# T1 and T3 of the seven-product pairs formed by accumulating DMA, and a fourth such pair per chunk

## The chip, the cores and the metric

The kernel runs on one core of a Trainium2 chip. The core has a matmul engine (TensorE; PE in the profile), an elementwise engine (VectorE; DVE), an activation engine (ScalarE; ACT), a general engine (GpSimd; POOL) and a queue engine that mostly issues DMAs (SyncE; SP). Each takes its own instructions in order and waits for the others by semaphores. The metric is the device time of one execution in microseconds; the time before is the median of three runs, 1666.11 us.

## The reference

One layer of a hybrid encoder on 256 rows of 2048 channels in float32: two attention branches, gated and merged, then a SwiGLU feed-forward part, then a norm. The change lies in the feed-forward part:

```
h2 = rmsnorm(x, ffn_norm_g)
x = x + (silu(h2 @ w_ffn_gate) * (h2 @ w_ffn_up)) @ w_ffn_down     # 2048 -> 5632 -> 2048
return rmsnorm(x, final_norm_g)
```

## The kernel before

A float32 product is made of three float32r products: each operand is split in a high part (ScalarE casts it, line 92) and a low part (VectorE subtracts, line 93), and `mm3` (lines 174 to 178) multiplies high by high, high by low and low by high. So each weight that is loaded costs a cast on ScalarE and a subtraction on VectorE before TensorE may use it.

The feed-forward part runs over 11 chunks of 512 hidden columns, in parts of 4, 4 and 3 chunks; after each part the down projection adds that part's share to the output. Inside a chunk, `hidden` (line 684) goes over 8 pairs of 128-row blocks of the 2048 input channels. For a pair there are four weight blocks of 128x512, stored side by side: the gate block of the first rows (g0), the up block of the second (u1), the up block of the first (u0) and the gate block of the second (g1).

A plain pair (`plain_weights`, line 638) loads these in two transfers of 512 KB, splits each in two operations of 128x1024 per engine, and multiplies in 24 matmuls of 512 columns (2 halves of the rows x 4 weights x 3). A pair in `SEVEN` (pairs 0, 2 and 4) takes the seven products of a Strassen-like scheme instead of eight, so 21 matmuls. For that the sums T1 = g0 + u0, T3 = u1 + u0, T2 = T1 + u1 and T4 = T2 + g1 of weights are formed on VectorE (lines 645 to 647) and split like weights; the sums of the activations (h2S) are made once. After the last such pair the seven accumulators are recombined (lines 699 to 703, four operations on VectorE), while the plain pairs that follow run on. `between` (line 691), called before pair 6, transposes the hidden values of the chunk before.

Slots are handed out by tile pools with tags: `raw` (6 slots, loaded weights), `w` (8 slots, split weights), `t` (5 slots, the sums, and the split g0, u1 and g1 of a seven-product pair). A slot is written again when its last reader is done. The order of each engine's instructions is set by a scheduler at build time, by its own timeline.

Of the kernel before, what the change touches and what calls it, by code (L numbers as in the profile page):

```python
# [8 lines left out]
F32 = mybir.dt.float32  # L9
F32R = mybir.dt.float32r  # L10
AF = mybir.ActivationFunctionType
ALU = mybir.AluOpType
AX = mybir.AxisListType

P = 128
# [14 lines left out]
G_END = 42  # L30

NF = 11
SEVEN = (0, 2, 4)

C_ID, C_DIST, C_COS, C_SIN, C_END = 0, 128, 512, 640, 768

# [2 lines left out]
def hybrid_block(ctx: ExitStack, tc: tile.TileContext, x, xT, gains, w_lat, w_kr, w_dqk, w_dv, w_g0, w_g1, b_gate,  # L39
                 w_qn, w_qr, w_kn, w_v, lq1, lk1, lq2, lk2, diff_norm_g, w_mla, w_diff, w_out, w_gu, w_fd,  # L40
                 final_norm_g, consts, out):
    nc = tc.nc
# [4 lines left out]
    wp = ctx.enter_context(tc.tile_pool(name="wp", bufs=1))  # L47
# [7 lines left out]
    def nm(s):  # L55
        n_tile[0] += 1
        return f"{s}_{n_tile[0]}"

    def lt(dt=F32, shape=(P, 2, S)):
        return up.tile(list(shape), dt, tag="L", name=nm("L"), bufs=48)  # L60
# [28 lines left out]
    def split(src, hi, lo, scale=None):  # L89

        if scale is None:
            nc.scalar.copy(hi, src)  # L92
            nc.vector.tensor_tensor(out=lo, in0=src, in1=hi.bitcast(F32), op=ALU.subtract)  # L93
        else:
            nc.scalar.activation(out=hi, in_=src, func=AF.Copy, scale=scale)
            nc.vector.scalar_tensor_tensor(out=lo, in0=src, scalar=scale, in1=hi.bitcast(F32),  # L96
                                           op0=ALU.mult, op1=ALU.subtract)
# [76 lines left out]
    def mm3(o, l, r, start, stop):  # L174

        nc.tensor.matmul(o, lhsT=l[0], rhs=r[0], start=start, stop=False)  # L176
        nc.tensor.matmul(o, lhsT=l[0], rhs=r[1], start=False, stop=False)  # L177
        nc.tensor.matmul(o, lhsT=l[1], rhs=r[0], start=False, stop=stop)  # L178
# [378 lines left out]
    for c in range(4):  # L557
        z, t = [lt(shape=(P, 512)) for _ in range(2)], [lt(shape=(P, 512)) for _ in range(2)]
# [12 lines left out]
    def sums_of(tp, gs):  # L571

        a, t = nt((P, 2, S)), nt((P, 4, P))
        for j in range(2):
            nc.scalar.activation(out=a[:, j], in_=tp[:, j], func=AF.Copy, scale=gs[j])
        a11, a12, a21, a22 = a[:, 0, 0:P], a[:, 1, 0:P], a[:, 0, P:S], a[:, 1, P:S]
        nc.vector.tensor_tensor(out=t[:, 0], in0=a21, in1=a22, op=ALU.subtract)
        nc.vector.tensor_tensor(out=t[:, 1], in0=a11, in1=a21, op=ALU.subtract)
        nc.vector.tensor_tensor(out=t[:, 2], in0=t[:, 0], in1=a11, op=ALU.subtract)
        nc.vector.tensor_tensor(out=t[:, 3], in0=a12, in1=t[:, 2], op=ALU.add)  # L580
        hi, lo = lt(F32R, (P, 4, P)), lt(F32R, (P, 4, P))
        split(t, hi, lo)
        return hi, lo

    x2ss = const.tile([P, 8], F32, name="x2ss")
    for c in range(4):
        o = project(mT, w_out, c)
        z = []
        for h in range(2):
            xr = nt()  # L590
            nc.sync.dma_start(out=xr, in_=x[0, h * P:(h + 1) * P, c * 512:(c + 1) * 512])
            t = lt(shape=(P, 512))
# [4 lines left out]
        for j0 in range(0, 4, 2):  # L597
# [5 lines left out]
            pair = 2 * c + j0 // 2  # L603
            if pair in SEVEN:
                h2S[pair] = sums_of(tp, gs)
# [10 lines left out]
    fp = ctx.enter_context(tc.tile_pool(name="fp", bufs=1, reuse_waits="tile"))  # L616
    fq = ctx.enter_context(tc.tile_pool(name="fq", bufs=1, space=bass.MemoryType.PSUM, reuse_waits="tile"))

    def bank(role, shape=(P, 512)):
        return fq.tile(list(shape), F32, tag=f"q{role}", name=nm("q"), bufs=1)  # L620

    def load(src):
        raw = wp.tile([P, 2, 512], F32, tag="raw", name=nm("raw"), bufs=6)
        nc.sync.dma_start(out=raw, in_=src)
        return raw
# [2 lines left out]
        return wp.tile([P, 2, 512], F32R, tag="w", name=nm("w"), bufs=8)  # L628

    def extra(dt=F32R):  # L630
        return fp.tile([P, 2, 512], dt, tag="t", name=nm("t"), bufs=5)

    def parts_of(src, alloc):
        hi, lo = alloc(), alloc()
        split(src, hi, lo)
        return [(hi[:, j], lo[:, j]) for j in range(2)]
# [3 lines left out]

    def seven_weights(src):

        a, b = load(src[:, 0:2]), load(src[:, 2:4])
        t13, t24 = extra(F32), extra(F32)
        nc.vector.tensor_tensor(out=t13, in0=a, in1=b[:, 0:1].broadcast_to([P, 2, 512]), op=ALU.add)
        nc.vector.tensor_tensor(out=t24[:, 0], in0=t13[:, 0], in1=a[:, 1], op=ALU.add)
        nc.vector.tensor_tensor(out=t24[:, 1], in0=t24[:, 0], in1=b[:, 1], op=ALU.add)
        w = {}
        w[1], w[3] = parts_of(a, extra)
        b21 = extra()  # L650
        split(b[:, 1], b21[:, 0], b21[:, 1])
        w[2] = b21[:, 0], b21[:, 1]
        w[5], w[7] = parts_of(t13, two)
        w[6], w[4] = parts_of(t24, two)
        return w
# [5 lines left out]
    def seven_products(q, pair, w, start, stop):  # L661

        hi, lo = h2S[pair]
        s1, s3, s2, s4 = [(hi[:, j], lo[:, j]) for j in range(4)]
        a0, a1 = h2T[2 * pair], h2T[2 * pair + 1]
        ls = {1: part_of(a0, 0), 2: part_of(a1, 0), 3: s4, 4: part_of(a1, 1), 5: s1, 6: s2, 7: s3}
        for i in (1, 5, 7, 6, 2, 3, 4) if start else (1, 3, 2, 5, 7, 6, 4):
            mm3(q[i], ls[i], w[i], start, stop and i in (1, 5, 6, 7))
# [15 lines left out]
    def hidden(c, between):  # L684

        pairs = len(h2T) // 2
        last = max(SEVEN) if SEVEN else None
        q, base = {}, None
        for p in range(pairs):
            if p == pairs - 2:  # L690
                between()
            if p in SEVEN:
                w = seven_weights(w_gu[c, p])
                if not q:
                    q = {i: bank(i) for i in (1, 5, 7, 6, 2, 3, 4)}
                seven_products(q, p, w, p == min(SEVEN), p == last)
                if p == last:
                    c1, v2, v3, d12, d22 = (sc() for _ in range(5))
                    nc.scalar.copy(c1, q[1])
                    nc.vector.tensor_tensor(out=v2, in0=c1, in1=q[6], op=ALU.add)  # L700
                    nc.vector.tensor_tensor(out=d12, in0=q[5], in1=v2, op=ALU.subtract)
                    nc.vector.tensor_tensor(out=v3, in0=q[7], in1=v2, op=ALU.add)
                    nc.vector.tensor_tensor(out=d22, in0=q[5], in1=v3, op=ALU.subtract)
                    base = ((c1, d12), (v3, d22))
                continue
            g0_, u1, u0, g1_ = plain_weights(w_gu[c, p])
            if 8 not in q:
                q[8] = bank(8)
            if not SEVEN and not p:
                q.update({i: bank(i) for i in (2, 3, 4)})  # L710
            for a, (wg, wu) in ((h2T[2 * p], (g0_, u0)), (h2T[2 * p + 1], (g1_, u1))):
                first_k = a is h2T[0]
                for h, (i, j) in enumerate(((2, 3), (4, 8))):
                    l = part_of(a, h)
                    end = a is h2T[-1]
                    mm3(q[i], l, wg, first_k, end)
                    mm3(q[j], l, wu, first_k or (j == 8 and SEVEN and p == 1 and a is h2T[2]), end)
        f = []
# [55 lines left out]
    for m in range(a, b):  # L774
        for j in range(4):
            if j % 2 == 0:
                raw = load(w_fd[3, m][:, j:j + 2])
# [104 lines left out]
```

## Time and profile before

| | us |
|---|---|
| median of three runs (lowest, highest) | 1666.11 (1664.88, 1667.57) |
| the profiled execution | 1665.36 |
| its span, first to last instruction | 1663.6 |
| PE busy in the span | 1648.0 (99%) |
| DVE busy | 1158.8 (70%) |
| ACT busy | 845.2 (51%) |
| POOL busy | 26.2 (2%) |

The engines work beside each other, so busy times don't add up. The chain of waits follows the work back from the last instruction and says which engine held the end at each moment. The windows cut the span in stretches and give each engine's busy time in them. A group row gives how often a form of an operation ran, its busy time and mean length, and the engine's idle time just before. Operations of one engine may overlap, so a mean length can be more than the distance from one start to the next, which the timeline shows.

### The profile page before, as it was taken

The numbers are of one execution on the slowest core, as the hardware profiler recorded it, in microseconds if no ns is written. First come the engines' busy times: TensorE is split into PE (matmuls) and PEld (weight loads), VectorE is DVE, ScalarE is ACT, GpSimd is POOL, SyncE is SP. The second block draws the span as 40 slices with busy tenths as digits, with TensorE's granted clock in tenths as the row PEclk, the third lists the DMA queues.
The fourth block names the chain that finished last, engine by engine and source line by source line (L and its number), as shares of the span: only waits on it lengthen the run. The fifth ranks groups of instructions, "written<-read, shape, count | busy, mean of one in ns | idle before, by whom it ended". The sixth has DMA issues, their size and how long they took to land.

```text
span 1663.6 us, 22367 instructions
## 1 busy us (share of the span) xinstructions
PE 1648.0 (99%) x8443; PEld 1407.1 (85%) x8443; DVE 1158.8 (70%) x1490; ACT 845.2 (51%) x1158; POOL 26.2 (2%) x49
## 2 busy tenths in 40 slices
PE   8999999999999999999999999999999999999998
PEld 7888888888888999998888788888888888888886
DVE  7676665666555766765656889975679885688865
ACT  6465554455444666565445555544445554445543
POOL 0000000010000000000000000000000000000010
PEclk9999999999999999999999999999999999999999
DMA  9655555466666545556766566666566655566662
GB/s 329 222 176 168 175 176 178 153 197 203 213 209 197 180 159 176 169 170 207 237 213 207 176 192 197 206 202 202 190 202 202 199 189 196 186 203 203 197 221 103
DMA packets 99133, 323.67 MB, mean 195 GB/s; under 512 B 10960, under 2 KB 17104, under 8 KB 99024
## 3 DMA queue, kind: packets, MB, share of 16 engines
q1 hardware_dynamic: 98880, 322.22, 58.7%
q8 instruction: 66, 1.08, 0.3%
q14 instruction: 43, 0.35, 0.1%
q10 hardware_dynamic: 144, 0.02, 0.0%
HBM read 315.91 MB, written 6.29 MB: 194 GB/s over the span
## 4 chain that ended last, share of the span: by engine, by line
PE 97%; DMA 1%; DVE 1%; ACT 0%; issue 0%; SPq 0%; ACTq 0%; POOLq 0%; POOL 0%; DVEq 0%
PE q L176 14%; PE q L177 14%; PE q L178 14%; PE mm L176 12%; PE mm L177 12%; PE mm L178 12%; PE mm L201 9%; PE mm L202 5%; PE ps L178 1%; PE ps L177 1%; PE ps L176 1%; PE q L677 1%; PE ps L108 1%; DMA raw<-in_w_dqk_dram 1%; DMA raw<-in_w_gu_dram 0%
## 5 line engine op out<-in xcount | busy, mean ns | idle before, releaser
L93 DVE TENSOR_TENSOR wlo<-raw,whi 128x1024 fp32r<-128x1024 f32 (+3 forms) x320 | 381.8, 1194 | 258.1 <-ACT whi L92 252.8
L92 ACT CAST whi<-raw 128x1024 fp32r<-128x1024 f32 (+3 forms) x320 | 329.0, 1028 | 349.0 <-PE mm L177 250.9
L176 PE MATMUL mm<-whi,L 128*128 128x512 f32 (+2 forms) x1080 | 384.0, 358 | 4.7 <-ACT whi L92 4.7
L178 PE MATMUL mm<-whi,L 128*128 128x512 f32 (+2 forms) x1080 | 385.8, 358 | 0.0
L177 PE MATMUL mm<-wlo,L 128*128 128x512 f32 (+2 forms) x1080 | 385.3, 357 | 0.0
L177 PE MATMUL q<-w,L 128*128 128x512 f32 x900 | 350.3, 390 | 0.0
L178 PE MATMUL q<-w,L 128*128 128x512 f32 x900 | 350.0, 390 | 0.0
L92 ACT CAST w<-raw 128x1024 fp32r<-128x1024 f32 x192 | 198.9, 1052 | 262.2 <-PE q L177 254.3
L176 PE MATMUL q<-w,L 128*128 128x512 f32 x900 | 315.0, 390 | 0.3 <-DVE L L96 0.3
L93 DVE TENSOR_TENSOR w<-raw,w 128x1024 fp32r<-128x1024 f32 x192 | 231.7, 1220 | 108.7 <-ACT w L92 108.7
L201 PE MATMUL mm<-L,whi 128*128 128x512 f32 x672 | 240.1, 398 | 0.6 <-DVE n L211 0.6
L176 PEld LDWEIGHTS mm<-whi,L 128*128 128x128 f32 x1080 | 204.3, 190 | 32.8 <-ACT whi L92 4.7
L178 PEld LDWEIGHTS mm<-whi,L 128*128 128x128 f32 x1080 | 204.4, 189 | 28.4
L177 PEld LDWEIGHTS mm<-wlo,L 128*128 128x128 f32 x1080 | 204.4, 189 | 28.3 <-DVE wlo L93 0.5
L176 PEld LDWEIGHTS q<-w,L 128*128 128x128 f32 x900 | 168.8, 188 | 35.2 <-PE q L178 0.7
L178 PEld LDWEIGHTS q<-w,L 128*128 128x128 f32 x900 | 169.0, 188 | 34.9
L177 PEld LDWEIGHTS q<-w,L 128*128 128x128 f32 x900 | 169.0, 188 | 34.6
L202 PE MATMUL mm<-L,wlo 128*128 128x256 f32 x672 | 189.4, 282 | 0.0
L201 PEld LDWEIGHTS mm<-L,whi 128*128 128x128 f32 x672 | 126.2, 188 | 28.5 <-DVE n L211 0.9
L202 PEld LDWEIGHTS mm<-L,wlo 128*128 128x128 f32 x672 | 127.0, 189 | 0.7
L93 DVE TENSOR_TENSOR w<-t,w 128x1024 fp32r<-128x1024 f32 x66 | 79.6, 1218 | 4.6 <-ACT w L92 4.0
L92 ACT CAST w<-t 128x1024 fp32r<-128x1024 f32 x66 | 68.5, 1051 | 25.2 <-PE q L177 12.6
(190 smaller groups left out, 1368.7 us busy)
## 6 DMA issues: line engine op xcount, KB each, us to landing
raw<-in_w_gu_dram SPq DMA_DIRECT2D x176, 512.0 KB, 4.6
raw<-in_w_fd_dram SPq DMA_DIRECT2D x88, 512.0 KB, 4.1
raw<-in_w_dqk_dram SPq DMA_DIRECT2D x64, 512.0 KB, 3.3
raw<-in_w_g_dram SPq DMA_DIRECT2D x64, 512.0 KB, 3.3
raw<-in_w_diff_dram SPq DMA_DIRECT2D x32, 512.0 KB, 3.3
raw<-in_w_mla_dram SPq DMA_DIRECT2D x32, 512.0 KB, 4.0
raw<-in_w_out_dram SPq DMA_DIRECT2D x32, 512.0 KB, 3.7
raw<-in_w_dv_dram SPq DMA_DIRECT2D x30, 512.0 KB, 3.2
```

The costliest lines, as they stand in the source:

```text
L92: nc.scalar.copy(hi, src)
L93: nc.vector.tensor_tensor(out=lo, in0=src, in1=hi.bitcast(F32), op=ALU.subtract)
L108: nc.tensor.transpose(tp[:, j, h * P:(h + 1) * P], blk[h], ident)
L176: nc.tensor.matmul(o, lhsT=l[0], rhs=r[0], start=start, stop=False)
L177: nc.tensor.matmul(o, lhsT=l[0], rhs=r[1], start=False, stop=False)
L178: nc.tensor.matmul(o, lhsT=l[1], rhs=r[0], start=False, stop=stop)
L201: nc.tensor.matmul(o[b], lhsT=ws[k][0][:, bs], rhs=a, start=k == 0, stop=False)
L202: nc.tensor.matmul(o[b][:, :S], lhsT=ws[k][1][:, bs], rhs=ah, start=False, stop=k == len(aT) - 1)
L677: nc.tensor.transpose(tp[:, j, h * P:(h + 1) * P], f[h][:, (2 * i + j) * P:(2 * i + j + 1) * P], ident)
```

## The change

Pair 5 joins the seven-product pairs. T1 and T3 are no longer added by VectorE: GpSimd issues a DMA that copies g0 and u1 into a tile of a new tag `u` (2 slots), and a second DMA that adds u0 from HBM to both halves of it. SyncE still loads g0 and u1 (512 KB) for their own splits, and of the other transfer only g1 (256 KB). T2 and T4 are still added by VectorE. The tag `t` goes from 5 slots to 4.

```diff
-SEVEN = (0, 2, 4)
+SEVEN = (0, 2, 4, 5)
...
     def extra(dt=F32R):
-        return fp.tile([P, 2, 512], dt, tag="t", name=nm("t"), bufs=5)
+        return fp.tile([P, 2, 512], dt, tag="t", name=nm("t"), bufs=4)
...
     def seven_weights(src):
 
-        a, b = load(src[:, 0:2]), load(src[:, 2:4])
-        t13, t24 = extra(F32), extra(F32)
-        nc.vector.tensor_tensor(out=t13, in0=a, in1=b[:, 0:1].broadcast_to([P, 2, 512]), op=ALU.add)
+        t13 = fp.tile([P, 2, 512], F32, tag="u", name=nm("u"), bufs=2)
+        nc.gpsimd.dma_start(out=t13, in_=src[:, 0:2])
+        nc.gpsimd.dma_start(out=t13, in_=src[:, 2:3].broadcast_to([P, 2, 512]), accum_op=ALU.add)
+        t24, a = extra(F32), load(src[:, 0:2])
+        b = wp.tile([P, 2, 512], F32, tag="raw", name=nm("raw"), bufs=6)
+        nc.sync.dma_start(out=b[:, 1], in_=src[:, 3])
         nc.vector.tensor_tensor(out=t24[:, 0], in0=t13[:, 0], in1=a[:, 1], op=ALU.add)
         nc.vector.tensor_tensor(out=t24[:, 1], in0=t24[:, 0], in1=b[:, 1], op=ALU.add)
```

In the changed kernel the lines below move down by three: its T2 and T4 are lines 649 and 650, the copy is line 644 and the add 645, the recombination lines 702 to 706.

On GpSimd, between the attention part and the end of the kernel, the kernel before has only the scale of the norm (lines 238, 239 and 612) and then, much later, the final gains (line 748):

```order
L446 MEMSET L_3515 128x512 [waits PE_49]
L238 TENSOR_SCALAR stat_9020<-stat_9017 128x2 [waits DVE_49,Activation_49]
L239 TENSOR_TENSOR stat_9021<-stat_9020,mhalf 128x2 [waits Pool_49]
L612 COPY r_9019<-stat_9021 128x2 [waits Pool_49]
L748 TENSOR_SCALAR L_14171<-L_14171 128x512 [waits DMAHW7_49,DVE_49,PE_49]
```

In the changed kernel the same place holds 88 DMAs. These are those of the third chunk: u_9776 is pair 0's, u_9866 pair 2's, u_9948 pair 4's and u_9994 pair 5's, and u_10150 and u_10240 belong to the chunk after it; DVE is a wait for VectorE, DMASW one for a DMA of this queue:

```order
L644 DMA u_9776<-in_w_gu_dram 128x1024 [waits DMASW5_49,DVE_49]
L645 DMA u_9776<-in_w_gu_dram 128x2x512 [waits DMASW0_49]
L644 DMA u_9866<-in_w_gu_dram 128x1024 [waits DMASW7_49,DVE_49]
L645 DMA u_9866<-in_w_gu_dram 128x2x512 [waits DMASW2_49]
L644 DMA u_9948<-in_w_gu_dram 128x1024 [waits DMASW1_49,DVE_49]
L645 DMA u_9948<-in_w_gu_dram 128x2x512 [waits DMASW4_49]
L644 DMA u_9994<-in_w_gu_dram 128x1024 [waits DMASW3_49,DVE_49]
L645 DMA u_9994<-in_w_gu_dram 128x2x512 [waits DMASW6_49]
L644 DMA u_10150<-in_w_gu_dram 128x1024 [waits DMASW5_49,DVE_49]
L644 DMA u_10240<-in_w_gu_dram 128x1024 [waits DMASW7_49,DVE_49]
```

Each copy waits for the VectorE operation that last read the slot, each add for its copy, and all stand in one line.

On VectorE, from pair 4 to the recombination, the kernel before has pair 4's sums and low parts and then the plain pairs 5 and 6 (t_9912 is T1/T3 of pair 4, t_9913 T2/T4, w_9966 and w_9972 pair 5):

```order
L93 TENSOR_TENSOR w_9925<-t_9912,w_9924 128x1024 [waits PE_49,Activation_49]
L647 TENSOR_TENSOR t_9913<-t_9913,raw_9910 128x512 [waits DVE_49]
L93 TENSOR_TENSOR t_9918<-raw_9908,t_9917 128x1024 [waits PE_49,Activation_49]
L93 TENSOR_TENSOR t_9921<-raw_9910,t_9921 128x512 [waits Activation_49]
L93 TENSOR_TENSOR w_9929<-t_9913,w_9928 128x1024 [waits Activation_49]
L93 TENSOR_TENSOR w_9966<-raw_9963,w_9965 128x1024 [waits DMAHW3_49,PE_49,Activation_49]
L93 TENSOR_TENSOR w_9972<-raw_9969,w_9971 128x1024 [waits DMAHW4_49,PE_49,Activation_49]
L93 TENSOR_TENSOR w_10020<-raw_10017,w_10019 128x1024 [waits DMAHW5_49,PE_49,Activation_49]
L700 TENSOR_TENSOR s_9954<-s_9953,q_9765 128x512 [waits PE_49,Activation_49]
```

In the changed kernel, from the last read of pair 2's u (u_9866) to the first read of pair 5's (u_9994):

```order
L93 TENSOR_TENSOR w_9884<-u_9866,w_9883 128x1024 [waits PE_49,Activation_49]
L93 TENSOR_TENSOR t_9880<-raw_9872,t_9880 128x512 [waits Activation_49]
L93 TENSOR_TENSOR w_9888<-t_9869,w_9887 128x1024 [waits PE_49,Activation_49]
L649 TENSOR_TENSOR t_9951<-u_9948,raw_9952 128x512 [waits DMAHW1_49,DMASW5_49,DVE_49]
L650 TENSOR_TENSOR t_9951<-t_9951,raw_9954 128x512 [waits DMAHW2_49,DVE_49]
L93 TENSOR_TENSOR w_9915<-raw_9912,w_9914 128x1024 [waits DMAHW7_49,PE_49,Activation_49]
L93 TENSOR_TENSOR w_9921<-raw_9918,w_9920 128x1024 [waits DMAHW0_49,PE_49,Activation_49]
L93 TENSOR_TENSOR t_9959<-raw_9952,t_9958 128x1024 [waits PE_49,Activation_49]
L93 TENSOR_TENSOR t_9962<-raw_9954,t_9962 128x512 [waits Activation_49]
L93 TENSOR_TENSOR w_9966<-u_9948,w_9965 128x1024 [waits PE_49,Activation_49]
L93 TENSOR_TENSOR w_9970<-t_9951,w_9969 128x1024 [waits PE_49,Activation_49]
L649 TENSOR_TENSOR t_9997<-u_9994,raw_9998 128x512 [waits DMAHW3_49,DMASW7_49,DVE_49]
```

Ten operations stand between the first and the last of these rows; the last waits for the add of pair 5 (DMASW), and pair 5's splits, then those of the plain pairs 6 and 7, follow behind it.

## Rows read from the trace of the kernel before

**Rows 1.** The page: the chain that ended last, by engine.
```profile
PE 97%; DMA 1%; DVE 1%; ACT 0%; issue 0%; SPq 0%; ACTq 0%; POOLq 0%; POOL 0%; DVEq 0%
```
**Rows 2.** Windows, three chunks between operations of line 700; first line names columns.
```profile
core 0: us, PE busy (x) PEld busy (x) DVE busy (x) ACT busy (x) POOL busy (x), PEclk, DMA share, GB/s
973.46:1014.94 41.48, 41.48 (x185) 34.35 (x184) 37.04 (x41) 23.75 (x27) 0.00 (x0) 1.00 0.63 200
1014.94:1057.62 42.68, 42.68 (x194) 35.32 (x193) 39.55 (x44) 23.50 (x28) 0.00 (x0) 1.00 0.61 198
1057.62:1099.84 42.22, 42.22 (x192) 34.95 (x191) 37.28 (x42) 23.46 (x27) 0.00 (x0) 1.00 0.62 198
sum 126.38, PE 126.38 PEld 104.61 DVE 113.87 ACT 70.71 POOL 0.00; mean PE 42.13 PEld 34.87 DVE 37.96 ACT 23.57 POOL 0.00
```
**Rows 3.** Timeline of PE: start, length, operation; six starts apart.
```profile
1009.68 0.39 PE L177 MATMUL q<-w,L 128*128 128x512 f32 x1
...
1011.04 0.39 PE L178 MATMUL q<-w,L 128*128 128x512 f32 x1
```
**Rows 4.** Timeline of DVE, small and large operations back to back.
```profile
990.24 0.68 DVE L723 TENSOR_TENSOR n<-s,q 128x512 f32<-128x512 f32 x1
990.84 0.69 DVE L647 TENSOR_TENSOR t<-t,raw 128x512 f32<-128x512 f32 x1
991.44 0.68 DVE L724 TENSOR_TENSOR s<-s,q 128x512 f32<-128x512 f32 x1
...
996.83 1.22 DVE L93 TENSOR_TENSOR w<-t,w 128x1024 fp32r<-128x1024 f32 x1
997.97 1.21 DVE L93 TENSOR_TENSOR t<-raw,t 128x1024 fp32r<-128x1024 f32 x1
999.11 1.21 DVE L93 TENSOR_TENSOR w<-t,w 128x1024 fp32r<-128x1024 f32 x1
1000.24 0.68 DVE L93 TENSOR_TENSOR t<-raw,t 128x512 fp32r<-128x512 f32 x1
```
**Rows 5.** Groups of DVE in these three chunks: count, busy, mean ns, idle before.
```profile
L93 DVE TENSOR_TENSOR w<-raw,w 128x1024 fp32r<-128x1024 f32 x30 | 36.1, 1218 | 7.2 <-ACT w L92 7.2
L93 DVE TENSOR_TENSOR w<-t,w 128x1024 fp32r<-128x1024 f32 x18 | 21.7, 1218 | 1.3 <-ACT w L92 1.2
L645 DVE TENSOR_TENSOR t<-raw,raw 128x1024 f32<-128x1024 f32 x9 | 11.0, 1223 | 1.5 <-DMA raw<-in_w_gu_dram 1.3
L93 DVE TENSOR_TENSOR t<-raw,t 128x1024 fp32r<-128x1024 f32 x9 | 10.9, 1216 | 0.0
L646 DVE TENSOR_TENSOR t<-t,raw 128x512 f32<-128x512 f32 x9 | 6.2, 685 | 0.1
```
**Rows 6.** Groups of ACT after 900 us: the two casts of a seven-product pair.
```profile
L92 ACT CAST w<-t 128x1024 fp32r<-128x1024 f32 x66 | 68.5, 1051 | 25.2 <-PE q L177 12.6 <-issue 6.0 <-DVE t L647 2.2
L92 ACT CAST t<-raw 128x512 fp32r<-128x512 f32 x33 | 20.4, 617 | 4.3 <-ACT t L92 3.9 <-PE q L177 0.4
```
**Rows 7.** The raw tile in the three chunks: SP's issues, and landing.
```profile
L624 SPq DMA_DIRECT2D raw<-in_w_gu_dram x46: 327/328/622, 975.3 to 1092.8; - x46
...
DMA to landing us min/median/max: 3.5/4.6/6.9
```
**Rows 8.** Window of the kernel's start, columns as in rows 2.
```profile
0.00:42.00 42.00, 36.70 (x164) 30.16 (x165) 30.21 (x54) 26.21 (x39) 2.96 (x6) 1.00 0.95 329
```
**Rows 9.** The tile x, four loads of 512 KB from 23.6 to 36.4 us.
```profile
DMA to landing us min/median/max: 5.9/7.9/9.8
```
**Rows 10.** Groups of POOL from 929 to 1570 us: its slowest operation there.
```profile
L239 POOL TENSOR_TENSOR stat<-stat,mhalf 128x2 f32<-128x2 f32 x1 | 0.7, 694 | 0.1
```

## The prediction

> **What bounds the kernel now.** I read the chain of waits first. TensorE holds 97% of it, DMA and VectorE 1% each [rows 1]. So the time is the sum of TensorE's columns, and a change pays where it takes matmuls away without making TensorE wait. Next the windows, cut at the gate/up part. Line 700 runs once per column chunk, right after the last seven-product pair, so the distance from one line 700 to the next is one chunk: 41.48, 42.68 and 42.22 us, 42.13 on average [rows 2]. In all three TensorE is busy from end to end at the full granted clock (1.00, the 2.4 GHz level), VectorE for 37.96 of 42.13 us, ScalarE for 23.57, and the DMA engines for 0.62 of the time. VectorE is thus the next limit, with 4.2 us to spare per chunk. GpSimd does nothing there.
>
> A matmul's own 390 ns is not its price, since matmuls overlap. The timeline has one start every 0.227 us (1009.68 to 1011.04 in six steps) [rows 3]. Check: 183 matmuls a chunk (3 pairs x 21 + 5 x 24) by 0.227 are 41.5 us; the 8 transposes fill the rest of 42.13. VectorE overlaps too: a 128x1024 operation lists 1.22 us but the next starts 1.14 us later (996.83, 997.97, 999.11, 1000.24), a 128x512 one costs 0.60 us (990.24, 990.84, 991.44) [rows 4]. I use these pitches.
>
> **The change, part by part.** *Pair 5 in seven products.* 24 matmuls become 21, in 11 chunks: 33 x 0.227 = 7.5 us off TensorE. All of it is on the chain if TensorE never waits. A chunk is then 42.13 - 0.68 = 41.45 us.
>
> *T1 and T3 by DMA.* VectorE loses the 128x1024 add (line 645, three per chunk). Counted for a chunk from its groups [rows 5]: today 22 operations of 128x1024 (10 plain low parts, 6 + 3 low parts of seven-product pairs, 3 adds). After it four such pairs have 3 each and four plain ones 2 each, 20. The 128x512 ones go up by 3, for the fourth pair. Sum: -2 x 1.14 + 3 x 0.60 = -0.48 us, so 37.5 of 41.45 us. VectorE stays just below TensorE, with 4.0 us to spare: the fourth pair is paid for by the adds that leave. ScalarE gains a cast of 1.05 and one of 0.62 us a chunk for that pair [rows 6] and stays near 25 of 41: free.
>
> *SP's queue* keeps its order; a seven-product pair loads 512 + 256 KB there instead of twice 512. SP waits on buffers, not on issuing, so this frees a little and costs nothing.
>
> *The new wait.* GpSimd now issues two transfers per pair: a copy of 512 KB, and, once that has landed, an add of another 512 KB into the same slot. The u tile has two slots, so the copy for pair 5 can't start until VectorE has read the u of pair 2 (low split, line 93). From there to VectorE's first use of pair 5's u (line 649 of the new kernel) stand ten operations, six of 128x1024 and four of 128x512: 9.2 us. Line 649 waits on the add, and queued behind it on VectorE are the low splits of pair 5, of pairs 6 and 7, and then the recombination; TensorE waits for those. Call the time from the release to the landed add T. As VectorE has 4.0 us to spare per chunk, and can give all of it to this one wait at best, **T may be 9.2 + 4.0 = 13.2 us before a chunk grows.** Beyond it a chunk is 37.5 + (T - 9.2). The gain of 0.68 us is eaten at T = 13.9. The same chain stands between pair 4 and pair 0 of the next chunk (9.8 us of VectorE work, but pair 5's wait lies inside it); elsewhere the distance is 14 us or more.
>
> *What is T?* The trace of before has no transfer issued by GpSimd and none that adds, so it is bounded from both sides. Nearest rows: a 512 KB load of w_gu by SP lands after 4.6 us (median; 3.5 to 6.9 in these chunks) and its issue takes 0.33 us [rows 7]; a 512 KB load under full DMA load (share 0.95, 329 GB/s) takes 7.9 us, at most 9.8 [rows 8, 9]. Low end: both as fast as the fastest w_gu load, 7.0 us, no wait at all. High end: a copy of 7.9 and an add of twice that, 23.7 us. I take the copy at 4.6; the add at 4.6 plus 1.6 us for a second stream of 512 KB at 329 GB/s, since it must also read its slot: 6.2; and 0.5 us for each of two issues with their semaphores, an estimate between SP's 0.33 and GpSimd's slowest small operation there, 0.69 [rows 10]. T = 11.8 us, 1.4 us inside the limit. So no wait is added, and the sum is -7.5 us.
>
> Sum: the profiled execution took 1665.36 us (its span 1663.6 and 1.8 around it); less 7.5 gives 1657.9. It lay 0.75 us under the median of the runs shown, 1666.11, so the median to expect is 1658.6, **1659 us**.
>
> Two rules are weighed. Rows 2 show the DMA engines at a share of 0.62 with 16 half-megabyte loads a chunk. The Trainium skill (Collectives: The Full Stack, "The bandwidth ceiling: the fold count and why AG ≠ RS ≠ AR") says that an add inside the DMA path runs at half a copy's rate because it needs two source reads. By that rule the add counts double in the share and the time is that of rival 3's 1.01; no run so far shows it. Rows 4 show VectorE with hardly a gap. The Trainium skill (SBUF — State Buffer, "Who interferes with whom") says that GpSimd can be kept from writing descriptors while VectorE runs in a two-port mode, and that a tensor_tensor takes only the read side of the shared port. By it the adds and splits here don't hold GpSimd off, and the sum stays; rival 2 prices the opposite.
>
> **The rivals.**
> 1. *The chain is late* (slower). Copy 6.9, add 6.9 + 1.6, issues 1.0: T = 16.4 us, 3.2 over the limit, by 11 chunks 35 us: 1666.1 - 7.5 + 35 = 1694. It decides from T = 13.9 on, only 2.1 us above my value. For it: w_gu loads already differ by 3.4 us among themselves, and VectorE already waits for raw at line 645 [rows 5]. Against it: GpSimd is idle, and half of the loads land in 4.6 us or less.
> 2. *GpSimd's issues wait for VectorE.* If each of the two is held back by one VectorE operation of 1.14 us, T = 14.1 and the result is 1666.1 - 7.5 + 11 x 0.9 = 1669; with less of a hold-up, no change. Against it: nothing in the trace shows GpSimd held off.
> 3. *The DMA engines become the bound.* A chunk now moves 14 half-megabytes on SP's queue, 4 copies and 4 adds: 22 for 16. Share 0.62 x 22/16 = 0.85; with each add counted double 26/16, 1.01; counted three times 30/16, 1.16. At 1.01 a chunk is 42.6 us and the result 1671; at 1.16 it is 48.9 us, +6.8 by 11, about 1741. For it: at a share of 0.95 landings already take 7.9 us [rows 8, 9]. Against: the first 42 us moved 329 GB/s, and 22 half-megabytes in 41.45 us are 278.
> 4. *Pairs 4 and 5 next to each other* (no change). They need 2 x (3 x 1.14 + 3 x 0.60) = 10.4 us of VectorE in 42 x 0.227 = 9.5 us of TensorE, and the four t slots hold one pair. If the 0.9 us isn't made up from the pairs around, a chunk loses 0.7 to 0.9 and the time is about 1666 to 1668. Against: behind them stand the plain pairs 6 and 7, which need 4.6 us of VectorE, with the recombination 7.0, in 48 x 0.227 = 10.9.
>
> **How the numbers follow.** Forecast, T up to 13.5 and faster by over 0.2%: 0.48. Rivals 2 and 4 with T near 13.9, within 0.2% (3.3 us, about what a measurement of this kernel can tell from no change): 0.13. Slower: the late chain 0.27 and DMA-bound 0.12, together 0.39. The range goes from 1656 (the 7.5 us and a little of the waits that line 645 leaves) to rival 1's 1694; beyond it lie the worse half of rival 3 and chains with T over 16.4, under 0.2. The likeliest case alone is 1656 to 1663.
>
> **What would show it.** Right: no idle of TensorE before q matmuls in the gate/up part, a chunk of 41.4 to 41.6 us from one recombination to the next, VectorE busy 37 to 38 of it, adds that land within 13 us of the release. Wrong: idle of VectorE at line 649 whose releaser is a DMA into u, a chunk over 42.1 us, two landings that sum to more than 13; or a DMA share over 0.95 with raw loads that land later than 6 us, which would be rival 3; or GpSimd's issues taking over 1 us each.

## The result and the profile after

The changed kernel takes **1721.38 us** (median; 1721.03 to 1722.43 in four runs) against 1665.77 us for the kernel before in the same comparison (1664.88 to 1667.57): a ratio of 1.0334, 95% interval 1.0316 to 1.0351. Slower by 56 us, where 7 us less was forecast. The execution whose profile follows took 1722.43 us, its span is 1720.7 us.

The chain of waits, by engine (page of the changed kernel; answers to [rows 1]):
```profile
PE 74%; issue 12%; DVE 6%; DMA 5%; ACT 1%; POOL 1%; SPq 0%; POOLq 0%; ACTq 0%; DVEq 0%
```
TensorE no longer sets the end alone. The windows of the same three chunks, again cut at the first VectorE operation of the recombination (columns as in [rows 2]):
```profile
983.50:1031.30 47.80, 44.83 (x181) 35.39 (x180) 37.18 (x43) 25.52 (x29) 6.32 (x8) 0.93 0.83 242
1031.30:1084.30 53.00, 44.68 (x187) 35.12 (x187) 37.40 (x44) 23.50 (x29) 8.28 (x9) 0.97 0.78 216
1084.30:1129.50 45.20, 40.52 (x170) 31.60 (x171) 37.22 (x44) 22.53 (x27) 7.10 (x8) 0.96 0.76 218
```
VectorE's work is 37.2 to 37.4 us a chunk, as forecast (37.5), but the chunk is 45 to 53 us long. TensorE idles 3 to 8 us in each, and the granted clock is below 1. The waits of line 649, VectorE's first use of a u tile, in the stretch 983 to 1130 us:
```profile
L649 DVE TENSOR_TENSOR t<-u,raw x11: 683/692/693, 991.3 to 1119.5; 128x512 f32<-128x512 f32 x11
its engine sat idle before it (us, times) until:
  issue: 19.9, 4
  DMA u<-in_w_gu_dram: 10.4, 2
  DMA raw<-in_w_gu_dram: 0.6, 1
```
That is 31 us in three chunks, 10.3 us each, and 37.3 + 10.3 = 47.6 us is nearly the whole chunk (48.7 on average). "Issue" is only a label here: each of those four waits ends 0.1 us after an add has landed, as the next rows show. They follow one such wait on VectorE and GpSimd (timelines; start, length, operation, idle before):
```profile
1050.04 1.22 DVE L93 TENSOR_TENSOR w<-u,w 128x1024 fp32r<-128x1024 f32 x1
...
1058.37 1.22 DVE L93 TENSOR_TENSOR w<-u,w 128x1024 fp32r<-128x1024 f32 x1
...
1069.23 0.69 DVE L649 TENSOR_TENSOR t<-u,raw 128x512 f32<-128x512 f32 x1 [8.51 <-issue]
...
1082.60 0.69 DVE L649 TENSOR_TENSOR t<-u,raw 128x512 f32<-128x512 f32 x1 [4.41 <-DMA u<-in_w_gu_dram]
```
```profile
1051.55 0.59 POOL L644 DMA_DIRECT2D u<-in_w_gu_dram  x1 [6.78 <-DVE w L93]
1057.15 1.18 POOL L645 DMA_DIRECT2D u<-in_w_gu_dram  x1 [5.01 <-DMA u<-in_w_gu_dram]
1059.88 0.59 POOL L644 DMA_DIRECT2D u<-in_w_gu_dram  x1 [1.55 <-DVE w L93]
1072.09 0.55 POOL L644 DMA_DIRECT2D u<-in_w_gu_dram  x1 [11.61 <-DVE w L93]
1072.63 1.25 POOL L645 DMA_DIRECT2D u<-in_w_gu_dram  x1
```
Pair 2's slot is free at 1051.26. GpSimd issues pair 5's copy 0.3 us later; it lands 5.3 us after its issue; the add is issued at 1057.15 and lands 12 us later. Line 649 starts at 1069.23: 18.0 us from release to use, 8.5 us of them idle. Pair 4's slot is free at 1059.59; pair 0's chain for the next chunk takes 22.9 us, partly because its add (1072.63) stands on GpSimd behind the next copy (1072.09), which waits for pair 5's slot. So pair 0 waits 4.4 us more, after pair 5's wait.

TensorE's clock fell as well, seven times from 994 to 1633 us, each time after TensorE had idled (for 1.5 to 3.3 us at a stretch). The first and last of these stretches and their sum (windows), then TensorE's timeline at the second one:
```profile
994.50:1001.33 6.83, 6.10 (x15) 4.46 (x14) 6.82 (x8) 6.06 (x8) 1.77 (x2) 0.50 0.67 144
...
1626.00:1632.83 6.83, 6.07 (x15) 4.78 (x15) 6.80 (x7) 5.99 (x7) 0.00 (x0) 0.50 0.36 108
sum 30.71, PE 28.28 PEld 21.60 DVE 30.57 ACT 25.36 POOL 7.71; mean PE 4.04 PEld 3.09 DVE 4.37 ACT 3.62 POOL 1.10
```
```profile
1042.45 0.80 PE L176 MATMUL q<-t,L 128*128 128x512 f32 x1 [3.33 <-DVE n L726]
1043.05 0.63 PE L177 MATMUL q<-t,L 128*128 128x512 f32 x1
1043.48 0.63 PE L178 MATMUL q<-t,L 128*128 128x512 f32 x1
1043.90 0.63 PE L176 MATMUL q<-t,L 128*128 128x512 f32 x1
```
At a granted 0.50 (the 1.2 GHz level) matmuls start 0.43 us apart in place of 0.227 [rows 3]. The seven stretches hold 73 of them (15 + 8 + 7 + 11 + 7 + 10 + 15): some 73 x 0.2 = 15 us lost at most.

The DMAs of the gate/up part (page: count, KB, median us to landing; the queue's packets, MB, share of 16 engines):
```profile
raw<-in_w_gu_dram SPq DMA_DIRECT2D x132, 512.0 KB, 6.1
u<-in_w_gu_dram POOLq DMA_DIRECT2D x88, 512.0 KB, 7.2
...
q0 software_dynamic: 18304, 46.14, 11.6%
```
A raw tile lands after 6.1 us where it was 4.6 [rows 7]. The u row mixes copies and adds: paired with their issues, the copies have a median of 5.6 us (3.8 to 12.0) and the adds of 8.8 us (5.3 to 12.0).

### The profile page after: what moved, and what is told of

Its sections match the earlier page's. It is cut to its first block, busy times and chain, and to the rows that moved or that the text cites. A ratio compares the mean times of both kernels' runs of the same rounds, so it can differ in the third digit from the quotient of the medians.

```text
span 1720.7 us, 22594 instructions
## 1 busy us (share of the span) xinstructions
PE 1666.1 (97%) x8410; PEld 1405.7 (82%) x8410; DVE 1159.1 (67%) x1506; ACT 861.3 (50%) x1183; POOL 106.2 (6%) x137
## 4 chain that ended last, share of the span: by engine, by line
PE 74%; issue 12%; DVE 6%; DMA 5%; ACT 1%; POOL 1%; SPq 0%; POOLq 0%; ACTq 0%; DVEq 0%
PE mm L177 12%; PE mm L178 12%; PE mm L176 12%; PE mm L201 9%; PE q L176 7%; PE q L177 7%; PE q L178 7%; PE mm L202 5%; DMA u<-in_w_gu_dram 3%; DVE w L93 3%; DMA raw<-in_w_gu_dram 1%; PE ps L177 1%; PE ps L178 1%; PE ps L176 1%; DVE t L93 1%
## 5 line engine op out<-in xcount | busy, mean ns | idle before, releaser
L177 PE MATMUL q<-w,L 128*128 128x512 f32 x856 | 338.2, 396 | 6.9 <-DVE w L93 6.8
L178 PE MATMUL q<-w,L 128*128 128x512 f32 x856 | 336.1, 394 | 0.0
L176 PE MATMUL q<-w,L 128*128 128x512 f32 x856 | 315.7, 399 | 18.9 <-ACT w L92 18.5
L93 DVE TENSOR_TENSOR w<-raw,w 128x1024 fp32r<-128x1024 f32 x170 | 204.9, 1220 | 84.7 <-ACT w L92 84.1
L92 ACT CAST w<-raw 128x1024 fp32r<-128x1024 f32 x170 | 175.2, 1050 | 158.8 <-PE q L177 145.5
L176 PEld LDWEIGHTS q<-w,L 128*128 128x128 f32 x856 | 161.7, 191 | 59.8 <-ACT w L92 26.8
L177 PEld LDWEIGHTS q<-w,L 128*128 128x128 f32 x856 | 163.0, 190 | 45.2 <-DVE w L93 11.1
L178 PEld LDWEIGHTS q<-w,L 128*128 128x128 f32 x856 | 163.1, 191 | 33.6
L649 DVE TENSOR_TENSOR t<-u,raw 128x512 f32<-128x512 f32 x44 | 30.4, 691 | 100.4 <-issue 54.9
L92 ACT CAST w<-u 128x1024 fp32r<-128x1024 f32 x44 | 46.1, 1049 | 96.1 <-DMA u<-in_w_gu_dram 69.0
```

## The experiments

In all, T is the time from the end of VectorE's last reading of a slot (line 93, `w<-u`) to the landed add of its next chain, and the hold is the time from line 649 to that last reading. Chunks are means of the eight distances inside the blocks of chunks, from recombination to recombination: 47.8 us in the changed kernel, 42.1 before. T and the hold are means over the chains of the same eight chunks. Each kernel was compared with the one before in the same runs (medians 1665.6 to 1666.4 us).

**1. The fourth pair alone.** `SEVEN = (0, 2, 4, 5)` in the kernel before.

> The kernel before with SEVEN = (0, 2, 4, 5): the fourth pair alone, all sums on VectorE, no accumulating DMA. Chain theory (the time was lost in the chain release, copy, add, use): no chain is left, so no waits on a landed add and no fall of the granted clock; VectorE's work per chunk becomes 37.96 + 4.49 = 42.45 us (one more seven-product pair of 6.93 us for a plain one of 2.44 us) against 41.45 us of TensorE, so a chunk of 42.5 to 43.5 us and 1668 to 1682 us in all. Rival, the fourth pair itself (pairs 4 and 5 side by side need more weights at once than TensorE can be given): 1700 us or more, with the waits before pair 5 still there. Rival, traffic: as chain, since no bytes are added.

1665.37 us, ratio 0.9992 (0.9983 to 1.0001): no difference, a little under the expected range. Second and third chunk (windows):
```profile
1020.00:1062.50 42.50, 42.26 (x190) 34.44 (x189) 42.18 (x48) 25.09 (x29) 0.00 (x0) 1.00 0.60 197
1062.50:1105.50 43.00, 42.15 (x190) 34.55 (x189) 42.17 (x50) 25.10 (x29) 0.00 (x0) 1.00 0.58 197
```
VectorE is busy 42.2 of 42.5 and 43.0 us: the bound has moved there, at the forecast 42.45. Pairs 4 and 5 side by side cost nothing that loses 56 us (here with five slots t; runs 3, 5 and 13 have the changed kernel's four).

**2. Accumulating DMA alone.** The changed kernel with `SEVEN = (0, 2, 4)`.

> The changed kernel with SEVEN = (0, 2, 4): T1 and T3 by accumulating DMA in the two slots u, no fourth pair. Chain theory: VectorE's work per chunk is 37.96 - 3.66 = 34.3 us, and between the release of a slot and the next use of it lie at least 10.6 us of VectorE's work; with the 7.8 us that VectorE can spare in a chunk of 42.13 us, a chain of 12 to 18 us is nearly hidden: 1664 to 1680 us. Rival, traffic (the added bytes slow the weight loads for everyone): three quarters of the loss of the changed kernel over TensorE's own time, 1666 + 0.75 x 63 = about 1710 us, with waits on the raw tiles as well as on u. Rival, GpSimd's one line (a copy that waits holds the next chain): 1680 to 1700 us.

1663.98 us, 0.9989 (0.9980 to 0.9999): the lower end of the chain theory. Line 649 waits 1.3 us in three chunks, for raw only. By runs 1 and 2 each half of the change alone costs nothing; together they are slow.

**3. The copy without the add.** The sum is left out: T1 and T3 are the copied columns alone.
```
-nc.gpsimd.dma_start(out=t13, in_=src[:, 2:3].broadcast_to(...), accum_op=ALU.add)
```


> The changed kernel without the accumulating DMA: T1 and T3 are the copied columns alone (the addition is left out), everything else as it is. Chain theory: release to landing falls from 10 to 23 us to 0.6 + 5 to 6 us, under the 9.2 us of VectorE's work that lie in between: the gaps ahead of t24 go, no fall of the clock, 1658 to 1664 us. Rival, traffic: half of the added writes and a third of the added reads are still there, so a third to a half of the loss stays, 1680 to 1690 us.

1657.38 us, 0.9948 (0.9933 to 0.9963). The forecast's -7.5 us is there once the chain is short (8.7 us less than before): TensorE's saving, and VectorE's work staying below it, were forecast rightly. The pages of this kernel and of the changed one (busy time, share, instructions), spans 1656.0 and 1720.7 us:
```profile
PE 1641.4 (99%) x8410; PEld 1400.4 (85%) x8410; DVE 1160.3 (70%) x1506; ACT 863.2 (52%) x1183; POOL 52.1 (3%) x93
```
```profile
PE 1666.1 (97%) x8410; PEld 1405.7 (82%) x8410; DVE 1159.1 (67%) x1506; ACT 861.3 (50%) x1183; POOL 106.2 (6%) x137
```
The same 8410 operations on TensorE: of the 64.7 us between the two spans 40.0 are its idle time and 24.7 more busy time. Up to 15 of the 24.7 are the clock. Some 7 more come from the stops themselves: the trace has 50 of them in place of 6, and the matmul before a stop shows its whole 0.39 us where the next start would have cut it to 0.227 [rows 3].

**4. Two chains a chunk.** Pairs 0 and 4 by DMA, pairs 2 and 5 on VectorE (`FORMED = (0, 4)`, the old add for the rest).

> Four seven-product pairs, with T1 and T3 of pairs 0 and 4 by accumulating DMA and those of pairs 2 and 5 on VectorE. Two chains a chunk in two slots: each slot has a whole chunk (about 41 us) from its release to its next use, and VectorE's work is 37.96 + 4.49 - 2.44 = 40.0 us a chunk against 41.45 us of TensorE. Chain theory: the chains are hidden, 1658 to 1668 us, the lower end if 1.4 us of spare VectorE time a chunk is enough. Rival, traffic: half of the added bytes remain and with them half of the loss, 1690 us. Rival, VectorE's coupling to ScalarE (it idled some 4 us a chunk before behind ScalarE's casts): 1680 us.

1665.04 us, 0.9995 (0.9985 to 1.0005): inside the range. The chains are hidden (the first use of a u tile waits 0.7 us in the mean), but nothing is gained; chunks vary from 40.7 to 43.9 us. Too little spare VectorE time (by the expectations 1.4 us a chunk, and 2.6 in run 13, which gains) is the likely reason; it is not shown.

**5. A third slot.** `u` with 3 slots, `s` with 6 in place of 8.

> The changed kernel with a third slot u (its 4 KB a partition taken from the tiles s, 6 in place of 8, which the front part feels if anything does). A slot is then released one seven-product pair earlier: between release and next use of pair 5's slot lie about 16 us of VectorE's work in place of 9.2, for pair 0 some 19 us. Chain theory: with 4 us to spare a chain of 12 to 18 us is hidden, no falls of the clock, 1657 to 1668 us. Rival, GpSimd's one line (copies and adds of four chains stand in one order there, each add waits for its copy): chains of four pairs still do not come in time, 1685 us or more. Rival, traffic: no change from 1721 us, since the bytes are the same.

1659.52 us, 0.9958 (0.9943 to 0.9973), faster than both kernels. Three chunks (windows), then line 649 and the u tile in them:
```profile
980.50:1103.10 122.60, 122.27 (x547) 100.77 (x546) 111.86 (x129) 73.66 (x84) 22.44 (x25) 1.00 0.92 281
```
```profile
L649 DVE TENSOR_TENSOR t<-u,raw x11: 685/692/694, 987.2 to 1091.4; 128x512 f32<-128x512 f32 x11
its engine sat idle before it (us, times) until:
  DMA raw<-in_w_gu_dram: 4.8, 2
...
DMA to landing us min/median/max: 5.5/8.8/16.0
```
The same bytes at a higher rate (281 GB/s, share 0.92), landings even later than in the changed kernel (8.8 us against 7.2, over these chunks), T 18.3 us in place of 16.1, and no wait for u. So neither traffic nor GpSimd's line sets the time: DMAs may be slow when they start a slot earlier.

**6. Every other pair.** `SEVEN = (0, 2, 4, 6)`.

> The changed kernel with SEVEN = (0, 2, 4, 6): the same four chains in the same two slots, but every other pair, so that each release and next use have about 11.8 us of VectorE's work between them in place of 9.2 for pair 5 and 15 for pair 2. Chain theory: with 4 us of spare a chain may take 15.8 us; those of the changed kernel took 10 to 23 us, 16 us in the median, so most of the loss goes but not all: 1660 to 1690 us. Rival, the sum of the chains counts and not the tightest distance (GpSimd's line, traffic): 1710 to 1725 us.

1722.07 us, 1.0337 (1.0315 to 1.0358): **a miss.** T was 16.8 us in the mean, 1 us over the 15.8 that I had allowed, and all was lost. The tightest single distance is thus the wrong measure. Two slots for four chains means that each slot is filled and read twice a chunk, however the pairs are spaced. Slot by slot: (18.6 + 7.2) + (15.2 + 5.4) = 46.4 us of T and hold for pairs 0 and 4, (17.7 + 9.4) + (15.5 + 6.1) = 48.7 for pairs 2 and 6, and the chunk is 47.9.

**7. A second step that doesn't add.** The second DMA without `accum_op`; the sum is left out, T1 and T3 are the second column alone.

> The changed kernel with the second DMA as a plain write of the same broadcast column in place of an accumulating one (T1 and T3 are then that column alone, the addition is left out): the chain has its two steps, its two issues and its waits, without the addition in the DMA. If the addition makes the second step long (8.8 us in the median against 5.6 us for the copy), it lands in 5 to 6 us, release to landing is 11 to 13 us, within 13.2 us: 1658 to 1672 us. If the second step is what costs, whatever it does, nothing is gained: 1700 us or more.

1690.37 us, 1.0147 (1.0131 to 1.0164): between the two expectations. The second step takes 6.4 us in the mean in place of 8.1; T is 13.8 us. So about half of the loss (1657 to 1690) is that there is a second step at all, and half (1690 to 1721) that it adds. The GpSimd queue of runs 3 and 7 (columns as above):
```profile
q0 software_dynamic: 6336, 23.07, 4.2%
```
```profile
q0 software_dynamic: 12672, 46.14, 8.5%
```
By share x span x 16, the copies take 1113 us of DMA engine time, a plain second step 1181 more, an accumulating one 2081 more: 1.8 times as much for the same bytes, in 11968 packets in place of 6336.

**8. The sum on GpSimd.** `nc.gpsimd.tensor_tensor` for the old add, four pairs, no DMA chain.

> Four seven-product pairs, T1 and T3 summed by GpSimd from the two raw tiles (one tensor_tensor of 128x1024 a pair in place of VectorE's), no accumulating DMA. VectorE's work a chunk is then 37.5 us as in the changed kernel, and the chain is raw, GpSimd, VectorE with no DMA in it. Chain theory: if GpSimd takes up to 4 us for one sum, the chain is covered and the time is 1657 to 1662 us, less than both kernels. Rival: GpSimd takes VectorE's access to SBUF while it adds, and VectorE's instructions get longer beside it; with 4 sums of 2 to 4 us a chunk on a VectorE at 37.5 of 41.45 us this reaches 1670 to 1700 us.

1687.51 us, 1.0126 (1.0111 to 1.0141): the rival. GpSimd's sum, and three of VectorE's groups from 960 us on (count, busy, mean ns, idle before):
```profile
L645 POOL TENSOR_TENSOR t<-raw,raw 128x1024 f32<-128x1024 f32 x44 | 124.2, 2823 | 1071.7 <-DMA raw<-in_w_gu_dram 897.4 <-DVE w L93 136.2 <-PE q L177 13.4
```
```profile
L93 DVE TENSOR_TENSOR w<-t,w 128x1024 fp32r<-128x1024 f32 x85 | 109.2, 1297 | 2.7 <-ACT w L92 2.2
L93 DVE TENSOR_TENSOR t<-raw,t 128x512 fp32r<-128x512 f32 x43 | 40.4, 940 | 0.0
L646 DVE TENSOR_TENSOR t<-t,raw 128x512 f32<-128x512 f32 x42 | 29.0, 691 | 61.7 <-POOL t L645 61.3
```
A sum takes 2.8 us in the mean. VectorE's low parts in `w` grew from 1218 [rows 5] to 1297 ns and the small ones in `t` from 0.68 us [rows 4] to 940 ns. These means hide two cases: in the trace ten of the 386 low parts from 925 us on take 2.9 to 3.4 us, each of them beside a sum on GpSimd, and the others are as long as before. The ten cost 21 us together, so VectorE's 61 us of waiting for GpSimd are the larger part.

**9. Reading u first.** `w[5], w[7] = parts_of(t13, two)` moved ahead of the splits of a.

> The changed kernel with one line moved: T1 and T3 are split into their weights first (right after the two additions that form T2 and T4), ahead of the splits of a and b, so that a slot u is held some 2.5 us from its first to its last use in place of 7 us in the mean (9.0, 10.9, 6.0 and 2.6 us for pairs 0, 2, 4 and 5). Same DMAs, same slots, same instructions. Slot theory (two slots serve four chains a chunk, so a chunk cannot be shorter than two turns of a slot, each release to landing plus hold): 2 x (16.1 + 2.5) = 37 us, under 41.45 us, so the waits go: 1657 to 1668 us. Rival, the add's own pace under load (GpSimd's line, DMA engines): no change, 1715 us or more. Rival, the order of the products: TensorE starts a pair with the weights of a, which now come later: 1670 to 1690 us with waits of TensorE on w at a pair's first matmul.

1722.80 us, 1.0335 (1.0318 to 1.0352), but **nothing was tested**: the scheduler at build time put VectorE's 1506 instructions, by operation and tile, into the very order they had, and the hold stayed at 6.8 us. Whether a shorter hold alone would do remains open.

**10. Both of 5 and 9.**

> Both at once: the third slot u and T1/T3 split first. If the chains are hidden by either alone, nothing is added by both: within 2 us of the better one, 1657 to 1661 us; what is left over 1657 us is then in the front part (fewer tiles s) and in ScalarE and VectorE's order. If chains still bind with three slots, up to 3 us better.

1661.17 us, 0.9967 (0.9956 to 0.9979), within 2 us of run 5. As in run 9 VectorE's order didn't change, so this is run 5 once more and tells nothing about the hold.

**11. One slot, three chains.** Run 2 with `u` at 1 slot.

> Three seven-product pairs by accumulating DMA, as in the run with SEVEN = (0, 2, 4), but with one slot u. Slot theory: a chunk cannot be shorter than three turns of the one slot, 3 x (release to landing 13 to 15 us + hold 8 us) = 63 to 69 us in place of 42.1 us; with eight such distances inside the three blocks of chunks and part of it in each block's first, 1664 + 8 x 24 + 3 x 12 = about 1890 us, 1850 to 1930 us. Distance rule of the prediction (each chain alone against VectorE's spare time of 7.8 us a chunk): the gain of time would be lost once, by the tightest chain only, 6 to 10 us a chunk, 1730 to 1760 us.

1798.68 us, 1.0796 (1.0765 to 1.0827): slower than the distance rule says, less than I expected of the slot theory. Consecutive turns of the slot, on VectorE and GpSimd (timelines):
```profile
1068.20 1.23 DVE L93 TENSOR_TENSOR w<-u,w 128x1024 fp32r<-128x1024 f32 x1 [0.46 <-ACT w L92]
1084.81 0.69 DVE L649 TENSOR_TENSOR t<-u,raw 128x512 f32<-128x512 f32 x1 [8.48 <-issue]
1086.15 1.22 DVE L93 TENSOR_TENSOR w<-u,w 128x1024 fp32r<-128x1024 f32 x1
1103.08 0.69 DVE L649 TENSOR_TENSOR t<-u,raw 128x512 f32<-128x512 f32 x1 [5.78 <-DMA u<-in_w_gu_dram]
```
```profile
1069.72 0.59 POOL L644 DMA_DIRECT2D u<-in_w_gu_dram  x1 [10.19 <-DVE w L93]
1074.97 1.18 POOL L645 DMA_DIRECT2D u<-in_w_gu_dram  x1 [4.65 <-DMA u<-in_w_gu_dram]
1087.66 0.59 POOL L644 DMA_DIRECT2D u<-in_w_gu_dram  x1 [11.52 <-DVE w L93]
```
In the whole run 30 of the 33 uses start 0.1 us or less after their add has landed. Three turns of T 14.4 + hold 4.1 are 55.7 us; the chunk is 56.3. What missed is the hold: a late chain finds the other splits done, and u is read at once (2.5 us for two of the three pairs), where I had 8.

**12. The 4 KB for a ninth w slot instead.** `s` with 6, `w` with 9, `u` with 2.

> The changed kernel with the same 4 KB taken from the tiles s (6 in place of 8), but given to a ninth slot w (split weights) and not to a third slot u. Slot theory (what counts is how many slots u serve the four chains): the DMA steps are as long as before, only the hold of a slot u can get shorter, by what ScalarE's cast of u waits for a free w: 1700 to 1722 us. Rival, the split weights (TensorE gives w free too late, and the chain is only where it shows): a ninth w recovers what the third u did, 1657 to 1670 us.

1698.25 us, 1.0189 (1.0174 to 1.0204), 2 us under the expected range. The memory taken from s is thus not what cured run 5. Pairs 2 and 5's slot now has 45.9 us of T and hold a chunk (48.0 in the changed kernel), the chunk is 45.3 and the clock falls twice, not seven times. With the ninth w slot the hold is 6.1 us in place of 6.9.

**13. One chain fewer.** `FORMED = (0, 2, 4)`: pair 5 on VectorE, two slots u, memory as in the changed kernel.

> Four seven-product pairs and two slots u, with T1 and T3 of pairs 0, 2 and 4 by accumulating DMA and those of pair 5 on VectorE. Slot theory: three chains a chunk in two slots, 1.5 turns of (release to landing 15 to 16 us + hold 7 to 8 us) = 33 to 36 us, under 41.45 us of TensorE; VectorE's work 37.5 + 1.2 = 38.8 us: no waits on u, no fall of the clock, 1656 to 1664 us, less than both kernels with no memory moved. Rival, the four pairs themselves with accumulating DMA in them (TensorE's and ScalarE's order around pairs 4 and 5): 1690 us or more.

**1658.82 us**, 0.9952 (0.9935 to 0.9968): faster than both kernels. Three chunks and their ends (windows):
```profile
976.00:1104.00 128.00, 127.48 (x570) 105.26 (x569) 117.03 (x136) 76.19 (x88) 15.92 (x18) 1.00 0.86 257
```
T is 16.6 us, as long as in the slow kernel, and in these chunks nothing waits for u.

Worked out for all with u by DMA (means in us; need = T + hold summed over the chains of a chunk in one slot, the fuller slot where they differ):

| run | chains / slots | T | hold | need per chunk | chunk | time |
|---|---|---|---|---|---|---|
| changed kernel | 4 / 2 | 16.1 | 6.9 | 48.0 | 47.8 | 1721.4 |
| 6 | 4 / 2 | 16.8 | 7.0 | 48.7 | 47.9 | 1722.1 |
| 9 | 4 / 2 | 16.3 | 6.8 | 48.2 | 48.2 | 1722.8 |
| 12 | 4 / 2 | 15.7 | 6.1 | 45.9 | 45.3 | 1698.3 |
| 7 | 4 / 2 | 13.8 | 6.9 | 43.2 | 44.5 | 1690.4 |
| 11 | 3 / 1 | 14.4 | 4.1 | 55.7 | 56.3 | 1798.7 |
| 13 | 3 / 2 | 16.6 | 8.3 | 37.4 | 40.9 | 1658.8 |
| 5 | 4 / 3 | 18.3 | 7.2 | 33.9 | 40.6 | 1659.5 |
| 2 | 3 / 2 | 14.9 | 8.0 | 34.3 | 42.1 | 1664.0 |

Where the need exceeds TensorE's 41.45 us, the chunk is within 1.3 us of it; where it does not, the chunk is TensorE's. How close the two come depends on where a chunk is cut: from one first use of a pair's u to the next it is 48.7 to 51.0 us in the changed kernel, where pairs 2 and 5's slot has its need of 48.0 and 2.3 us more in which landed tiles stand unused. So the need is a floor. Where a slot is never free, its T and holds must fill the chunk, so the upper rows alone prove little. What shows the cause are the runs that changed the count of slots or chains: 5 and 13 are fast at a longer T, 11 is slow at a shorter one.

## Why the prediction was wrong

- **TensorE's saving and VectorE's work: right.** 1657.4 us in run 3 against a forecast of 1658.6, and 1658.8 in run 13, which forms all sums; VectorE 37.2 to 37.4 us a chunk against 37.5.
- **The step that failed is T:** "T = 11.8 us, 1.4 us inside the limit. So no wait is added". T was 16.3 us in the mean for pair 5 and 16.1 over all four, and VectorE idled 6.2 us a chunk ahead of pair 5's first use. For pair 5 the copy took 5.4 us in the mean, not 4.6, and the add 10.2, not 6.2; the two issues and their waits took 0.7, not 1.0. What I mis-sized is the landing time under the new load. I took it from loads at a share of 0.62, though rival 3 itself put the new share at 0.85 and rows 8 and 9 had 7.9 us at 0.95. The change adds 8 transfers of 512 KB to a chunk's 16 and takes away about 2, and raw tiles landed later with it: after 4.6 us before, 4.9 with the copies alone (run 3), 5.8 with a plain second step (run 7) and 6.1 in the changed kernel.
- **What the adding itself costs** I had put at 1.6 us. By run 7 it is 1.7 us in the means (8.1 against 6.4) and 2.9 between the medians (8.8 against 5.9); pair 5's second step took 8.8 us even without adding. So most of the 4.0 us by which its add was late is not the adding. The Trainium skill (Collectives: The Full Stack, "The bandwidth ceiling: the fold count and why AG ≠ RS ≠ AR") has the reduce step of a ring at half the rate of the copy step, since its add needs two source reads; run 7 gives 1.8 times the DMA engine time, so the trace nearly agrees, though the landing time grew by less.
- **The limit was wrong as well.** "T may be 9.2 + 4.0 = 13.2 us" looked at pair 5's wait alone and let pair 0's lie inside it. With T = 16.3 the prediction's own formula gives a chunk of 44.6 us; it measured 47.8, and pair 0 waits some 5 us of its own in the mean. For two slots the limit is half a chunk less the hold, in the mean over *all* chains: 41.45 / 2 - 6.9 = 13.8 us, with 16.1 measured. Run 6 shows it: the distance rule allowed 15.8 us there, T was 1 us over, and nothing was gained.
- **Rival 1 was what happened** (a late chain, in this place, T = 16.4), and 1694 us its price. The 27 us beyond it I put down to pair 0's wait and the clock; no run separates the two. The fall of the granted clock had no term at all.
- **Rival 2:** not seen. Copies issue 0.3 us after the release (0.6 in the mean: pair 2's stand behind pair 0's add), in 0.6 us, adds in 1.2 us. The 1.2 us is over the 1 us that I named as a sign, but run 5 has it too and is fast. GpSimd did hold an add back, but behind its own waiting copy (2 us at 1070 us), not by VectorE.
- **Rival 3:** refuted by run 5, which moves the same bytes faster.
- **Rival 4:** runs 1 and 13 show no cost beyond VectorE's own work.

Open: why pair 5's second step is the longest of the four in the changed kernel and in run 7, and whether shorter holds alone would rescue two slots.

## What to carry to other kernels

Before giving a chain of transfers a small ring of slots, add up, per slot and period, fill time plus hold for every turn, at landing times under the new load. If the sum is over the period, the period grows to the sum at least. Spacing the users did not help here; one slot more or one chain fewer did. Both halves of a change can be free and their union slow: here one raised the number of chains, and the other gave each chain its need.

## What the runs showed of the hardware

- Two dependent 512 KB transfers by GpSimd, a copy and an add, took 16.1 us in the mean from release to landing in the changed kernel (DMA share 0.76 to 0.83 in the three chunks; singly 9.8 to 23.9 us), and 18.3 us in run 5 (share 0.92). The Trainium skill (DMA: Bandwidth & Descriptors, "Anatomy of one DMA — SWDGE (gpsimd) path") gives 2.0 us plus bytes over 436 GB/s, by which an estimate for 512 KB is 3.2 us. The fastest copy of any run agrees (3.2 us in run 3, whose median is 4.7); in the changed kernel the fastest took 3.8 and the median was 5.6.
- A wait of TensorE cost more than its length: seven falls to a granted 0.50 (the 1.2 GHz level), each behind an idle stretch, took up to 15 us on top of 40 us of idle time.
- A GpSimd sum of 128x1024 fp32 took 2.8 us in the mean where VectorE's takes 1.22 [rows 5]. Ten of 386 low parts on VectorE took some 2.2 us longer beside such a sum; the others did not change.
